# The first feed-forward stage in block form, with the norm's scales on x from the opening on

## The chip, the cores and the metric

The kernel runs on one core of a Trainium2 chip, in one launch. The metric is the time of the launch in microseconds (us) on the device. TensorE (PE in the profile) multiplies, VectorE (DVE) and ScalarE (ACT) work element by element, GpSimd (POOL) does little here beside issuing transfers, and SyncE (SP) issues the transfers of the weights. Each of them executes its own instructions in the order in which they were recorded.

## The reference

A decoder trunk of two layers over 256 tokens with 1024 features, all in float32. Each layer adds four things to the residual h: half a SwiGLU (`ffn1`), a mixer (an S5 state space beside differential attention), a cross attention into 256 memory tokens, and half a second SwiGLU (`ffn2`).

```python
def swiglu(x, w_gate, w_up, w_down):
    return (jax.nn.silu(x @ w_gate) * (x @ w_up)) @ w_down
...
    for l in range(DEPTH):
        h = h + 0.5 * swiglu(rms_norm(h, ffn1_norm[l]), ffn1_w_gate[l], ffn1_w_up[l], ffn1_w_down[l])
        h = h + hybrid_mixer(rms_norm(h, mix_norm[l]), ...)
        h = h + memory_cross_attention(rms_norm(h, xattn_norm[l]), rms_norm(mem, mem_norm[l]), ...)
        h = h + 0.5 * swiglu(rms_norm(h, ffn2_norm[l]), ...)
    return rms_norm(h, final_norm)
```

The inner width of a SwiGLU is 2816. `rms_norm` multiplies by a gain for each feature and by 1/rms for each token. The gain can go onto the rows of the weight or onto the columns of x; the factor of the token is applied behind the product.

## The kernel before

**Split products.** A float32 product is made of three products of a shorter float type: each operand is split into a high part (`whi`, `xh`, made by ScalarE) and a low part (`wlo`, `xl`, the rest, made by VectorE), and TensorE adds hi x hi, lo x hi and hi x lo in PSUM. Every weight that TensorE uses therefore passes ScalarE and then VectorE first.

**The weight stream.** The weights lie in HBM in the order of use, in units of 128x1024 (`stream_plan` lists them). SyncE loads a unit into a `raw` buffer (4 of them), ScalarE makes `whi`, VectorE `wlo` (5 buffers of each). A unit whose norm gain goes onto the weight is split in two halves with the gain as a factor (`split_unit`: forms with `raw,gains`); one without a gain is split whole (`split_whole`). How far the stream runs ahead is bounded by the 5 buffers: a unit's `whi` can begin when TensorE is through with the unit five earlier.

**A feed-forward stage.** The 2816 columns are 11 chunks of 256 gate and 256 up columns. A chunk is four weight units of type A (`P` in the tables below, 12 matmuls of 128x512 each: 2 token tiles x 2 halves x 3 products), and its result (`z`, `sg`) is gated, transposed, split (`gT`) and multiplied by two units of down weights (`D`, 12 matmuls each) some chunks later.

**The pair.** Three of the four stages, all but the first, put two chunks together (`ffn2` does so twice): with two token tiles, two halves of the features and two chunks, a 2x2 block product is made of seven block products instead of eight (`PAIR`: Q3, Q1, Q7, Q6, Q2, Q5, Q4, each two units of 6 matmuls). VectorE forms sums of x blocks (`combos`: `xf`, `ef`, `el`) and of weight blocks in place (`add_block`: `blkX`, `blkY`), and puts the products together (`qs`). Sums of x blocks need the gain on x, so in these stages the residual's preparation scales x with it (`split_gain`, four pieces of 128x128, as the gain is another column for each), and the weights carry none. The order of a stage is a table written out by hand (`SECOND_ONE` for `ffn1`; P chunk, D down rows, S a pair's product):

```python
SECOND_ONE = (
    "P0 P0 P0 P0 P1 P1 P1 P1 P4 D0 P4 D0 "
    "S2 P4 P4 S2 D1 P5 S2 D1 P5 S2 P5 P5 S2 D4 P6 S2 D4 P6 S2 P6 D5 P6 "
    "D5 D3 P7 D3 P7 D2 P7 D2 P7 D6 P8 D6 P8 P8 P8 D7 P9 P9 P9 P9 D7 P10 P10 P10 P10 D8 D8"
)
```

Layer 0's first stage instead goes through `ffn`, eleven plain chunks with the gain on the weights.

**Work beside the stages.** The recording layer is written as tasks (generators) over a clock of estimated costs (`Clock`); the clock decides only in which order instructions are recorded on each engine. `ssm_small` makes the state space's small coefficients for both layers (a chain of about 84 VectorE operations on 128x32, names `sp`, `ex`, `th`, `n`, `fr`, `x`, `pw`, `pr`, `fz`). `tables` makes a layer's larger tables (`tab_states`: `bbar`, `V`, `VT`; `tab_turns`: `ang`, `rnd`, `rot`, `dt`; `tab_out`: `W`, `ks`, `dd`); they use the same buffers (`tA` to `tD`) as the pair's blocks. `setup_mem`, `setup_bias` and `setup_lam` prepare the memory's tiles, the bias and the lambdas. `START` holds the clock times at which `ssm_small` (first value) and the set-up tasks (second) begin. In layer 1 the tables are started when the stage's last pair product has been recorded; in layer 0, which has no pair in `ffn`, from the start of the small chain.

**The opening** (`opening`) covers the first chunk: x comes in by halves (`h` tiles), is transposed by TensorE and split without a gain; the first three weight units are split in halves between these steps; `junk` is the square sum for the norm. The dummy matmuls `pz` keep TensorE busy until the data are there.

Of the kernel before, what the change touches and what calls it, by code (L numbers as in the profile page):

```python
# [11 lines left out]
F32 = mybir.dt.float32  # L12
F32R = mybir.dt.float32r
BF16 = mybir.dt.bfloat16
I32 = mybir.dt.int32
AF = mybir.ActivationFunctionType
# [3 lines left out]
L = 2  # L20
# [11 lines left out]
LAG = 2  # L32
# [13 lines left out]
MMW = 0.8  # L46
START = (45.0, 34.0)
PACE = 2.6
# [63 lines left out]
def stream_plan():  # L112

    plan = []
    for l in range(L):
        def ffn(nm):
            for j in range(NCH):
                for kp in range(4):
                    plan.append((nm + "_gu", l, 4 * j + kp, "A", (nm, l, 2 * kp), 4 if j == 0 and len(plan) >= 4 else 1))
                if j >= LAG:  # L120
                    for f in range(2):
                        plan.append((nm + "_dn", l, 2 * (j - LAG) + f, "B", None, 1))
            for n in range(2 * (NCH - LAG), 2 * NCH):
                plan.append((nm + "_dn", l, n, "B", None, 2 * LAG))

        def second(nm):
            for kind, j, k in second_items(nm):
                if kind == "P":
                    plan.append((nm + "_gu", l, 4 * j + k, "A", None, 4 if j == 0 else 1))
                elif kind == "D":  # L130
                    plan.append((nm + "_dn", l, 2 * j + k, "B", None, 1))
                else:
                    _, loads, operand, add = PAIR[k]
                    for u in range(2):
                        n = [4 * (j + a) + 2 * b + u for _, a, b in loads]
                        plan.append((nm + "_gu", l, n, "S", ((nm, l, j), u, [x[0] for x in loads], operand, add), 1))
            for n in range(2 * (NCH - LAG), 2 * NCH):
                plan.append((nm + "_dn", l, n, "B", None, 2 * LAG))
# [4 lines left out]

        ffn("ffn1") if l == 0 else second("ffn1")
        for c in range(4):
# [239 lines left out]
class Trunk:  # L385
# [319 lines left out]
    def opening(self, evac):  # L705
# [6 lines left out]
        def tr(t, n):  # L712
            p = self.transpose4(self.h[t], [512 * n + 128 * i for i in range(4)])
            o = [a[:, 4 * n:4 * n + 4, :].rearrange("p a b -> p (a b)") for a in self.x[t]]
            self.split(o[0], o[1], p)
            self.tp_done(p)
# [163 lines left out]

    def ffn(self, nm, preps, tail):
        bank = {}
        gT = {}
        accs = None

        def evac(j):
            def f(t, ps):
                c = self.c
                if j:
                    yield tasks[j - 1][t]  # L890
                c.cur.t = max(c.cur.t, self.rt[t])
                sg = self.gp.tile([128, 256], F32, tag="sg", name="sg")
                self.a.activation(sg, ps[:, 0:256], AF.Silu, scale=self.r[t])
                self.v.scalar_tensor_tensor(sg, ps[:, 256:512], self.r[t], sg, op0=ALU.mult, op1=ALU.mult)
                self.mm_done()
                yield
                if j not in bank:
                    yield from self.tp_wait()
                    bank[j] = self.tpt()
                    n = 0  # L900
                else:
                    n = 1
                p = bank[j]
                for f in range(2):
                    o = f * 256 + t * 128
                    self.p.transpose(p[:, o:o + 128], sg[:, f * 128:f * 128 + 128], self.ident)
                if n == 1:
                    hl = self.s4t([128, 2, 512], F32R, name="gT")
                    self.split(hl[:, 0, :], hl[:, 1, :], p)
                    self.tp_done(p)  # L910
                    gT[j] = hl

            return f

        def xs(j, f, t):
            o = f * 256 + t * 128
            return gT[j][:, 0, o:o + 128], gT[j][:, 1, o:o + 128]

        tasks = {}
        for j in range(NCH):  # L920
            if j == 0 and preps is None:
                tasks[j] = self.opening(evac(j))
            else:
                tasks[j] = self.project(nm + "_gu", self.x, evac(j), preps if j == 0 else None)
            if j >= LAG:
                i = j - LAG
                self.c.wait(*tasks[i])
                if accs is None:
                    accs = [self.acc_main(), self.acc_main()]
                for f in range(2):  # L930
                    u = self.unit(nm + "_dn")
                    for t in range(2):
                        self.mm_b(accs[t], *xs(i, f, t), u, i == 0 and f == 0, False)
                    self.free_unit()
        for i in range(NCH - LAG, NCH):
            self.c.wait(*tasks[i])
        base = NCH - LAG
        return self.blocks(nm + "_dn", accs, lambda t, k: xs(base + k // 2, k % 2, t), 2 * LAG, False, True, tail)

    def combos(self, E):  # L940
# [29 lines left out]

    def ffn_second(self, nm, preps, tail, then=None):

# [133 lines left out]
        for kind, j, k in second_items(nm):  # L1106
            if kind == "P":
                if j == 0:
                    if k == 0:
                        tasks[0] = self.project(nm + "_gu", self.x, evac(0, None), preps)  # L1110
                    if k < 3:
# [262 lines left out]
    def tables(self, l, z, tb, first):  # L1374

        st = self.c.spawn(self.chain(first, self.tab_states(l, z, tb), self.tab_turns(l, z, tb)), START[0] if l == 0 else None)
        return st, self.c.spawn(self.chain(st, self.tab_out(l, z, tb)), START[0] if l == 0 else None)

# [440 lines left out]
    def setup(self):  # L1819
# [8 lines left out]
        win = lambda u, s: nc.sync.dma_start(self.raw[u][:, s], io["wst"][u][:, s])  # L1828
        xin(0, lo)
        xin(1, lo, nc.scalar)  # L1830
        nc.scalar.dma_start(self.gains, io["gains"])
        win(0, lo)
# [72 lines left out]
    def run(self):  # L1905
# [5 lines left out]
        small = c.spawn(self.ssm_small(z), START[0])  # L1911
        tables = self.tables(0, z, tb, small)
        c.spawn(self.chain(self.setup_mem(0), self.setup_mem(1), self.setup_bias(), self.setup_lam()), START[1])
        for l in range(L):
            if l == 0:
                preps = self.ffn("ffn1", preps, prep(0.5))
            else:
                tb, tables = {}, []
                preps = self.ffn_second("ffn1", preps, prep(0.5), lambda: tables.extend(self.tables(l, z, tb, None)))
            preps = self.mixer(l, preps, tb, tables, prep(1.0))  # L1920
            preps = self.cross(l, preps, prep(1.0, ("ffn2", l)))
            if l == L - 1:
                self.fn = self.s4t([128, 1024], name="fn")
                self.g.dma_start(self.fn, self.io["final_norm"].to_broadcast([128, 1024]))
            preps = self.ffn_second("ffn2", preps, prep(0.5, ("ffn1", l + 1)) if l < L - 1 else (lambda t, acc: self.final(t, acc, 0.5)))
        c.wait(*preps)
# [69 lines left out]
```

## Time and profile before

| | |
|---|---|
| median of 3 runs | 1193.92 us (1193.57 to 1193.97) |
| profiled execution | 1193.89 us |
| its span, first to last instruction | 1192.1 us |
| PE busy | 1182.4 us (99%) |
| DVE busy | 909.7 us (76%) |
| ACT busy | 707.1 us (59%) |
| POOL busy | 46.7 us (4%) |
| granted TensorE clock | 0.999 |

Times in the profile count from the first instruction. A row of the timeline reads: start in us, duration in us, engine, line, operation, output<-inputs, shapes, count, and in brackets the idle time before it with what ended it. Rows of the same kind that follow each other are merged, and the durations of neighbours overlap, so the price of an instruction in a full queue is the distance of starts and not its duration. A row of windows gives, for each stretch, the busy time and number of instructions of PE, PEld, DVE, ACT and POOL, then the granted clock, the share of the DMA engines and GB/s. Layer 0's first feed-forward stage runs from about 7 us to 208 us of the span, layer 1's from 601 us to 794 us. A line number such as L293 is that of a helper through which all of an engine's operations go, so the names of the tiles tell where an instruction belongs.

### The profile page before, as it was taken

What the parts mean: (1) busy time and instruction counts of PE and PEld (TensorE: products, weight loads), DVE (VectorE), ACT (ScalarE), POOL (GpSimd) and SP (SyncE); (2) the same over time, 40 slices, a digit from 0 to 9 for tenths busy, and PEclk for the clock granted to TensorE, in tenths of its full rate; (3) what the DMA queues carried; (4) which work ended last, traced back from release to release, by engine and by line L of the source; (5) the groups of instructions that cost most, each with busy time, mean ns of one, the idle gap of its engine ahead of it and who ended that gap; (6) DMA issues with size and microseconds to landing.
All of it is one profiled execution on the core that took longest, in us unless ns stands there. A gap on an engine that the chain in (4) does not pass through costs nothing.

```text
span 1192.1 us, 17474 instructions
## 1 busy us (share of the span) xinstructions
PE 1182.4 (99%) x6571; PEld 967.8 (81%) x6571; DVE 909.7 (76%) x1331; ACT 707.1 (59%) x1141; POOL 46.7 (4%) x104
## 2 busy tenths in 40 slices
PE   9999999999999999999999999999999999999997
PEld 7888788877888888888888887888778888888886
DVE  5799676598767688889588985766978575888885
ACT  6665554656866566565466644455767665656553
POOL 1200001000100000000000000010001000000000
PEclk9999999999999999999999999999999999999999
DMA  8656545644544465474557364556436445836542
GB/s 276 227 185 208 156 165 170 195 126 140 177 160 141 159 229 213 142 263 126 176 199 266 123 199 150 176 154 180 150 101 208 150 149 176 305 120 240 183 125 87
DMA packets 59973, 210.90 MB, mean 177 GB/s; under 512 B 7168, under 2 KB 8288, under 8 KB 59888
## 3 DMA queue, kind: packets, MB, share of 16 engines
q1 hardware_dynamic: 56304, 202.92, 52.1%
q0 software_dynamic: 2000, 5.24, 1.6%
q10 hardware_dynamic: 1584, 1.62, 0.6%
q8 instruction: 51, 0.84, 0.3%
q14 instruction: 34, 0.28, 0.1%
HBM read 207.00 MB, written 1.05 MB: 175 GB/s over the span
## 4 chain that ended last, share of the span: by engine, by line
PE 97%; ACT 1%; issue 0%; DMA 0%; DVE 0%; POOLq 0%; POOL 0%; ACTq 0%; DVEq 0%
PE mm L369 50%; PE acc L369 33%; PE tp L369 10%; PE tp L380 5%; DMA gains<-in_gains 0%; ACT junk L330 0%; ACT whi L330 0%; DVE h L293 0%; DVE ang L293 0%; ACT on L330 0%; ACT z L330 0%; DVE wlo L293 0%; POOLq L1992 0%; ACT xh L330 0%; POOL rstd L353 0%
## 5 line engine op out<-in xcount | busy, mean ns | idle before, releaser
L369 PE MATMUL mm<-whi,xh 128*128 128x512 f32 x736 | 295.3, 401 | 1.1 <-ACT whi L330 1.0
L293 DVE TENSOR_TENSOR wlo<-raw,whi 128x1024 fp32r<-128x1024 f32 (+1 forms) x228 | 248.0, 1108 | 51.8 <-ACT whi L330 51.1
L369 PE MATMUL mm<-whi,xl 128*128 128x512 f32 x736 | 287.5, 391 | 0.0
L369 PE MATMUL mm<-wlo,xh 128*128 128x512 f32 x736 | 286.9, 390 | 0.3 <-DVE wlo L293 0.3
L330 ACT ACTIVATE whi<-raw 128x1024 fp32r<-128x1024 f32 (+1 forms) x228 | 214.0, 967 | 54.6 <-PE acc L369 25.6
L293 DVE SCALAR_TENSOR_TENSOR wlo<-raw,gains,whi 128x512 fp32r<-128x512 f32 x280 | 198.7, 746 | 53.0 <-ACT whi L330 50.9
L369 PE MATMUL acc<-whi,gT 128*128 128x512 f32 (+1 forms) x704 | 235.3, 395 | 0.0
L330 ACT ACTIVATE whi<-raw,gains 128x512 fp32r<-128x512 f32 x280 | 184.0, 714 | 10.6 <-PE mm L369 4.6
L369 PEld LDWEIGHTS mm<-whi,xh 128*128 128x128 f32 x736 | 138.2, 188 | 31.7 <-ACT whi L330 1.6
L369 PEld LDWEIGHTS mm<-whi,xl 128*128 128x128 f32 x736 | 138.1, 188 | 29.6 <-DVE xl L293 0.3
L369 PEld LDWEIGHTS mm<-wlo,xh 128*128 128x128 f32 x736 | 138.5, 188 | 26.5 <-DVE wlo L293 1.0
L369 PEld LDWEIGHTS acc<-whi,gT 128*128 128x128 f32 x704 | 132.0, 188 | 26.5
L369 PE MATMUL acc<-wlo,gT 128*128 128x512 f32 (+1 forms) x352 | 136.8, 389 | 0.0
L369 PE MATMUL mm<-whi,mem 128*128 128x512 f32 x256 | 92.4, 409 | 0.2
L330 ACT ACTIVATE z<-mm,rstd 128x256 f32<-128x256 f32 (+1 forms) x70 | 37.8, 547 | 71.7 <-PE mm L369 71.1
L369 PEld LDWEIGHTS acc<-wlo,gT 128*128 128x128 f32 x352 | 66.3, 188 | 12.1
L330 ACT ACTIVATE gT<-tp 128x512 fp32r<-128x512 f32 x44 | 26.4, 599 | 60.4 <-PE tp L380 60.3
L369 PEld LDWEIGHTS mm<-whi,mem 128*128 128x128 f32 x256 | 48.1, 188 | 12.7 <-ACT z L330 1.6
L293 DVE TENSOR_TENSOR wlo<-blkX,whi 128x1024 fp32r<-128x1024 f32 x40 | 48.6, 1220 | 9.9 <-ACT whi L330 9.9
L330 ACT ACTIVATE whi<-blkX 128x1024 fp32r<-128x1024 f32 x40 | 42.0, 1055 | 19.5 <-PE mm L369 7.0
L369 PE MATMUL mm<-wlo,mem 128*128 128x512 f32 x128 | 50.2, 393 | 0.0
L293 DVE TENSOR_TENSOR gT<-tp,gT 128x512 fp32r<-128x512 f32 x44 | 30.3, 688 | 24.6 <-ACT gT L330 24.6
(261 smaller groups left out, 1583.4 us busy)
## 6 DMA issues: line engine op xcount, KB each, us to landing
raw<-in_wst SPq DMA_DIRECT2D x342, 512.0 KB, 4.1
blkX<-in_wst SPq DMA_DIRECT2D x10, 512.0 KB, 4.6
blkP<-in_wst SPq DMA_DIRECT2D x10, 512.0 KB, 7.9
blkY<-in_wst SPq DMA_DIRECT2D x10, 512.0 KB, 9.0
blkQ<-in_wst SPq DMA_DIRECT2D x10, 512.0 KB, 9.6
raw<-in_wst SPq DMA_DIRECT2D x4, 256.0 KB, 5.7
mem<-in_mem POOLq DMA_DIRECT2D x2, 512.0 KB, 4.3
uq<-z ACTq DMA_DIRECT2D x8, 128.0 KB, 5.8
```

The source lines that it names most:

```text
L293: r = getattr(self.e, name)(*a, **k)
L330: r = self.e.activation(out, in_, func, **k)
L369: r = self.e.matmul(out, lhsT, rhs, **k)
L380: r = self.e.transpose(out, in_, ident)
```

## The change

Layer 0's first stage is made as the other three are, with chunks 2 and 3 as a pair; the function `ffn` is removed, and `ffn_second` takes its name. In detail:

- The plan lists the stage by `second`; none of its weight units has a gain, so outside the opening they are split whole.
- The opening's transposed x is split with the gains (`split_gain`) instead of without. For that the gains are fetched first on ScalarE's queue, ahead of the second tile of x.
- `tables` of layer 0 is started by the stage's last pair product, as in layer 1, and then waits for `ssm_small` if that is not through.
- `START` goes from (45, 34) to (60, 110).

```diff
-START = (45.0, 34.0)
+START = (60.0, 110.0)
...
-                    plan.append((nm + "_gu", l, 4 * j + k, "A", None, 4 if j == 0 else 1))
+                    plan.append((nm + "_gu", l, 4 * j + k, "A", None, 4 if j == 0 and len(plan) >= 4 else 1))
...
-        ffn("ffn1") if l == 0 else second("ffn1")
+        second("ffn1")
...
-            o = [a[:, 4 * n:4 * n + 4, :].rearrange("p a b -> p (a b)") for a in self.x[t]]
-            self.split(o[0], o[1], p)
+            self.split_gain(self.x[t], n, p, "ffn1", 0)
...
-    def ffn_second(self, nm, preps, tail, then=None):
+    def ffn(self, nm, preps, tail, then=None):
...
-                        tasks[0] = self.project(nm + "_gu", self.x, evac(0, None), preps)
+                        evac0 = evac(0, None)
+                        tasks[0] = self.opening(evac0) if preps is None else self.project(nm + "_gu", self.x, evac0, preps)
...
-        st = self.c.spawn(self.chain(first, self.tab_states(l, z, tb), self.tab_turns(l, z, tb)), START[0] if l == 0 else None)
-        return st, self.c.spawn(self.chain(st, self.tab_out(l, z, tb)), START[0] if l == 0 else None)
+        st = self.c.spawn(self.chain(first, self.tab_states(l, z, tb), self.tab_turns(l, z, tb)))
+        return st, self.c.spawn(self.chain(st, self.tab_out(l, z, tb)))
...
         xin(0, lo)
+        nc.scalar.dma_start(self.gains, io["gains"])
         xin(1, lo, nc.scalar)
-        nc.scalar.dma_start(self.gains, io["gains"])
...
         small = c.spawn(self.ssm_small(z), START[0])
-        tables = self.tables(0, z, tb, small)
...
-            if l == 0:
-                preps = self.ffn("ffn1", preps, prep(0.5))
-            else:
-                tb, tables = {}, []
-                preps = self.ffn_second("ffn1", preps, prep(0.5), lambda: tables.extend(self.tables(l, z, tb, None)))
+            tb, tables = {}, []
+            preps = self.ffn("ffn1", preps, prep(0.5), lambda: tables.extend(self.tables(l, z, tb, None if l else small)))
```

How instructions move is seen at two places. The first is VectorE where the small chain begins. Before, it stands among half splits with gains of plain chunks (`wlo<-raw,gains,whi`):

```order
L293 SCALAR_TENSOR_TENSOR wlo<-raw,gains,whi 128x512 x5
L293 TENSOR_SCALAR sp<-sp 128x32
L293 TENSOR_SCALAR ex<-sp 128x32
L293 TENSOR_SCALAR ex<-ex 128x32 x2
L293 SCALAR_TENSOR_TENSOR ex<-ex 128x32 x2
L293 TENSOR_SCALAR ex<-ex 128x32
L293 SCALAR_TENSOR_TENSOR ex<-ex 128x32
L293 SCALAR_TENSOR_TENSOR wlo<-raw,gains,whi 128x512 x2
L293 SCALAR_TENSOR_TENSOR ex<-ex 128x32 x5
```

Now it stands inside the pair, behind the block addition and the first split for product Q6 (`blkX`):

```order
L283 TENSOR_TENSOR blkX<-blkX,blkP 128x1024
L283 TENSOR_TENSOR wlo<-raw,whi 128x1024
L283 TENSOR_TENSOR wlo<-blkX,whi 128x1024
L283 TENSOR_SCALAR sp<-sp 128x32
L283 TENSOR_SCALAR ex<-sp 128x32
L283 TENSOR_SCALAR ex<-ex 128x32 x2
L283 SCALAR_TENSOR_TENSOR ex<-ex 128x32 x2
L283 TENSOR_SCALAR ex<-ex 128x32
L283 SCALAR_TENSOR_TENSOR ex<-ex 128x32
L283 TENSOR_TENSOR wlo<-blkX,whi 128x1024
L283 TENSOR_TENSOR wlo<-raw,whi 128x1024
L283 SCALAR_TENSOR_TENSOR ex<-ex 128x32 x5
```

The chain has kept its operations, and what stands between them is now the pair's. It ends behind the pair's last product; 75 of its 84 operations stand ahead of the split of chunk 6's third unit.

The second place is ScalarE in the opening. Before, a gain goes onto each weight half, and x is split in pieces of 512 columns:

```order
L1827 DMA h_109<-in_x 128x512
L1831 DMA gains<-in_gains 128x90
L330 ACT_TABLE_LOAD
L330 ACTIVATE warm<-zero 128x1
L330 ACTIVATE xh<-tp 128x512
L330 ACTIVATE whi<-raw,gains 128x512
L330 ACTIVATE xh<-tp 128x512
L330 ACTIVATE whi<-raw,gains 128x512 x3
L330 ACTIVATE junk,ssq<-h_108 128x1024
```

Now:

```order
L1761 DMA gains<-in_gains 128x90
L1758 DMA h_109<-in_x 128x512
L320 ACT_TABLE_LOAD
L320 ACTIVATE warm<-zero 128x1
L320 ACTIVATE xh<-tp,gains 128x128 x4
L320 ACTIVATE whi<-raw 128x512
L320 ACTIVATE xh<-tp,gains 128x128 x4
L320 ACTIVATE whi<-raw 128x512 x3
L320 ACTIVATE junk,ssq<-h_108 128x1024
```

The two transfers have changed places, the gain has gone from the weights to x, and each piece of x has become four. The places of the steps are the same.

More of the change, by code (lines that the diff above doesn't have):

```diff
@@ L115, in stream_plan @@
     for l in range(L):
[L116 to L124, printed above, removed]
         def second(nm):
@@ L878, in final @@
         yield
[L881 to L900, printed above, removed]
-                else:
[L902 to L938, printed above, removed]
     def combos(self, E):
@@ L1911, in run @@
         small = c.spawn(self.ssm_small(z), START[0])
-        tables = self.tables(0, z, tb, small)
         c.spawn(self.chain(self.setup_mem(0), self.setup_mem(1), self.setup_bias(), self.setup_lam()), START[1])
         for l in range(L):
-            if l == 0:
-                preps = self.ffn("ffn1", preps, prep(0.5))
-            else:
-                tb, tables = {}, []
-                preps = self.ffn_second("ffn1", preps, prep(0.5), lambda: tables.extend(self.tables(l, z, tb, None)))
+            tb, tables = {}, []
+            preps = self.ffn("ffn1", preps, prep(0.5), lambda: tables.extend(self.tables(l, z, tb, None if l else small)))
             preps = self.mixer(l, preps, tb, tables, prep(1.0))
@@ L1924, in run @@
                 self.g.dma_start(self.fn, self.io["final_norm"].to_broadcast([128, 1024]))
-            preps = self.ffn_second("ffn2", preps, prep(0.5, ("ffn1", l + 1)) if l < L - 1 else (lambda t, acc: self.final(t, acc, 0.5)))
+            preps = self.ffn("ffn2", preps, prep(0.5, ("ffn1", l + 1)) if l < L - 1 else (lambda t, acc: self.final(t, acc, 0.5)))
         c.wait(*preps)
```

## The prediction

> **What bounds the kernel now.** I read the page first, then who waited for whom on TensorE, then the timelines of VectorE, ScalarE and TensorE at the three places that the change touches. The page:
>
> ```profile
> span 1192.1 us, 17474 instructions
> PE 1182.4 (99%) x6571; PEld 967.8 (81%) x6571; DVE 909.7 (76%) x1331; ACT 707.1 (59%) x1141; POOL 46.7 (4%) x104
> PE 97%; ACT 1%; issue 0%; DMA 0%; DVE 0%; POOLq 0%; POOL 0%; ACTq 0%; DVEq 0%
> ```
>
> TensorE is busy for all but 9.7 us, and the chain that ended last is 97% PE. Its waits (engine, line, for whom; us in total, times, longest):
>
> ```profile
> PE pz L369 <- DVE zero L293: 1.2, 1, 1.2
> PE mm L369 <- ACT whi L330: 1.0, 1, 1.0
> PE mm L369 <- DVE wlo L293: 0.3, 1, 0.3
> PE tp L380 <- DMA h<-in_x: 0.2, 1, 0.2
> ```
>
> All four lie in the opening; behind it TensorE never waits. So the time is TensorE's row of work: a matmul less is a gain, and any new wait of TensorE is a loss in full. The profiled execution took 1193.89 us, 1.8 us more than its span and 0.03 under the median of 1193.92; I sum against 1193.89.
>
> **The matmuls removed.** Two plain chunks are 8 units of 12 matmuls, 96; the pair is 14 units of 6, 84. Each is 128x512 (TensorE's timeline in the same stage of layer 1):
>
> ```profile
> 687.59 0.39 PE L369 MATMUL mm<-wlo,xh 128*128 128x512 f32 x1
> 690.33 0.39 PE L369 MATMUL acc<-wlo,gT 128*128 128x512 f32 x1
> ```
>
> These two matmuls start 2.74 us apart with eleven others between them, 0.228 each. 12 x 0.228 = 2.7 us less. The transposes stay the same in number: the gain is 2.7.
>
> **The pair beside the small chain.** The operand sums, block additions and extra splits of the pair are VectorE and ScalarE work. Layer 1's first stage has had the same pair, and TensorE waits nowhere there, so by itself this costs nothing. Its cover is VectorE's lead over TensorE. What layer 1 does not have is the state space's chain of small operations (128x32, `ssm_small`), which now stands inside the pair. In the order of the changed kernel it begins right behind the split of the first half of product Q6, and 75 of its 84 operations stand ahead of the split of chunk 6's third unit (`P6`, between the last product, Q4, and the first block of chunk 5's down rows), where the delay is greatest. VectorE executes in order, so each of them delays every split behind it. Layer 1's VectorE over that stretch:
>
> ```profile
> 653.43 1.22 DVE L293 TENSOR_TENSOR wlo<-blkX,whi 128x1024 fp32r<-128x1024 f32 x1
> 655.56 1.23 DVE L293 TENSOR_TENSOR wlo<-blkX,whi 128x1024 fp32r<-128x1024 f32 x1 [0.91 <-ACT whi L330]
> 660.51 1.23 DVE L293 TENSOR_TENSOR wlo<-blkQ,whi 128x1024 fp32r<-128x1024 f32 x1 [1.44 <-ACT whi L330]
> 662.14 0.69 DVE L293 TENSOR_TENSOR qs<-tp,qs 128x512 f32<-128x512 f32 x1 [0.40 <-PE tp L369]
> 678.42 0.48 DVE L293 SCALAR_TENSOR_TENSOR qs<-qs,rstd 128x256 f32<-128x256 f32 x1
> 682.28 1.22 DVE L293 TENSOR_TENSOR wlo<-raw,whi 128x1024 fp32r<-128x1024 f32 x1
> 683.42 0.87 DVE L293 SCALAR_TENSOR_TENSOR qs<-qs,rstd 128x256 f32<-128x256 f32 x2
> ```
>
> Count from 654.65, the end of Q6's first split. VectorE is through with that third unit (the split at 682.28) at 683.42, 28.8 us later. Taking off the three idle pieces (2.75) and the `qs` at 678.42, which the changed order puts behind it (0.4), its work is 25.6 us. TensorE asks for that split at 687.59, 32.9 us after the start. So 7.3 us are free, and the small chain must fit into them.
>
> What one small operation costs is in layer 0 of the profile, where the same chain stands among half splits (VectorE's busy time in a window, then rows of it):
>
> ```profile
> 51.86:88.18 36.32, 36.32 (x170) 29.94 (x169) 32.88 (x117) 19.72 (x32) 0.24 (x1) 1.00 0.67 224
> 51.86 0.28 DVE L293 TENSOR_SCALAR sp<-sp 128x32 f32<-128x32 f32 x1
> 51.94 0.22 DVE L293 TENSOR_SCALAR ex<-sp 128x32 f32<-128x32 f32 x1
> L293 DVE SCALAR_TENSOR_TENSOR ex<-ex 128x32 f32<-128x32 f32 x16 | 3.1, 191 | 0.5
> 54.74 1.08 DVE L293 SCALAR_TENSOR_TENSOR ex<-ex 128x32 f32<-128x32 f32 x5
> 55.74 1.22 DVE L293 TENSOR_TENSOR wlo<-raw,whi 128x1024 fp32r<-128x1024 f32 x1
> 73.72 0.21 DVE L293 TENSOR_TENSOR pw<-mag,cs 128x32 f32<-128x32 f32 x1
> 74.72 1.21 DVE L293 TENSOR_TENSOR wlo<-raw,whi 128x1024 fp32r<-128x1024 f32 x1
> 48.53 3.40 DVE L293 SCALAR_TENSOR_TENSOR wlo<-raw,gains,whi 128x512 fp32r<-128x512 f32 x5 [0.96 <-ACT whi L330]
> 78.16 0.48 DVE L293 SCALAR_TENSOR_TENSOR sg<-mm,rstd,sg 128x256 f32<-128x256 f32 x1 [1.47 <-ACT sg L330]
> ```
>
> Five that feed each other take 1.00 us (0.20 each); the eight from 73.72, side by side, 1.00 (0.125 each). Over the window: 117 instructions, 31 of them large: 17 half splits of 0.66, 4 whole ones of 1.14, 4 gate products of 0.4, four 512-wide lows of 0.6 and two of 0.45 for the lambdas, 20.7 us in all; idle, 1.47 at 78.16 and 0.5 in two shorter waits. That leaves 13.7 us for 86, 0.16 each. So 75 take 12.0, and 12.0 - 7.3 = 4.7 us of wait for TensorE. Behind it the lead comes back without further loss: the splits stand closer, nine small operations are left, and after the pair there is room even with the memory's four splits (0.6 each) and the lambda chain moved there, since layer 1's VectorE waits there for ScalarE:
>
> ```profile
> 726.37 1.23 DVE L293 TENSOR_TENSOR wlo<-raw,whi 128x1024 fp32r<-128x1024 f32 x1 [11.02 <-ACT whi L330]
> ```
>
> Bounds: at 0.09 each (51.86 to 51.94, the nearest pair that does not wait for its forerunner) 75 fit but for nothing, 0; at 191 ns, the mean duration of one, 14.3 - 7.3 = 7.0. I take 4.7, by the window, which is the same chain on the same engine.
>
> The Trainium skill has a rule that speaks for the lower end: Perfetto Trace Analysis, section "Optimizing Scalar/DVE Operations", puts the overhead of an instruction on VectorE at about 60 ns on SBUF. With 32 columns at the 0.96 GHz that VectorE: DVE Perf Modes gives (section "The TRN2 errata"), this is an estimate of 93 ns, 75 take 7.0 and TensorE would not wait at all. The window's 0.16 disagrees.
>
> **The opening.** x is now scaled by the gains as it is split: four pieces of 128x128 in place of one of 128x512, on ScalarE and on VectorE. Rows: eight pieces from the stage where layer 0's second feed-forward begins, then the opening as it is.
>
> ```profile
> 413.88 2.27 ACT L330 ACTIVATE xh<-tp,gains 128x128 fp32r<-128x128 f32 x8 [6.18 <-PE tp L380]
> 415.06 2.25 DVE L293 SCALAR_TENSOR_TENSOR xl<-tp,gains,xh 128x128 fp32r<-128x128 f32 x8 [1.15 <-ACT xh L330]
> 6.52 0.72 ACT L330 ACTIVATE whi<-raw,gains 128x512 fp32r<-128x512 f32 x1 [0.88 <-DMA gains<-in_gains]
> 7.30 0.50 PE L369 MATMUL mm<-whi,xh 128*128 128x512 f32 x1 [1.01 <-ACT whi L330]
> 11.24 0.60 ACT L330 ACTIVATE xh<-tp 128x512 fp32r<-128x512 f32 x1 [0.64 <-PE tp L380]
> 13.07 0.60 ACT L330 ACTIVATE xh<-tp 128x512 fp32r<-128x512 f32 x1 [0.19 <-PE tp L380]
> 13.56 4.39 ACT L330 ACTIVATE whi<-raw,gains 128x512 fp32r<-128x512 f32 x7
> 15.12 0.50 PE L369 MATMUL mm<-wlo,xh 128*128 128x512 f32 x1 [0.28 <-DVE wlo L293]
> gains<-in_gains ACTq DMA_DIRECT2D x1, 45.0 KB, 5.3
> ```
>
> Four pieces hold ScalarE 1.1 us where one took 0.5, so +0.6 for each. Of the two in x's second half the first loses 0.2 to the idle piece at 13.07, so the third weight unit (13.56) starts 1.0 later; without its gain it is 0.1 shorter, and TensorE's wait, which ended at 15.12, ends 0.9 later. With 0.1 from VectorE's longer low parts: +1.0. The start itself: the first weight split (6.52) waited for the gains, whose transfer now goes first on ScalarE's queue, while x's second tile goes second. If the gains land early, up to 0.4 is won; if they again take 5.3 us from an issue 0.44 earlier, the pieces begin at about 6.0, and the first matmul, 1.1 + 0.7 later, starts 0.5 late. Range -0.4 to +1.5, and I take +1.0.
>
> **Moved.** Without gains the first stage's weights are split whole, which is less work; nothing has to cover it. The tables (`tab_states`, `tab_turns`, `tab_out`) wait for the pair, as they do in layer 1, where TensorE waits for none. There is one difference: their last four operations (`dd`, `ks`) now stand on VectorE between the two halves of the first preparation's x, ahead of the mixer. Layer 1 has them before the residual, and a gap at the place where they would now press:
>
> ```profile
> 784.17 0.42 DVE L293 TENSOR_TENSOR dd<-dc,cst 16x256 f32<-16x256 f32 x1
> 784.69 0.42 DVE L293 TENSOR_TENSOR ks<-ks,dd 16x256 f32<-16x256 f32 x1
> 793.29 2.08 DVE L293 SCALAR_TENSOR_TENSOR wlo<-raw,gains,whi 128x512 fp32r<-128x512 f32 x3 [0.81 <-ACT whi L330]
> ```
>
> Four at 0.45 are 1.8 us, 0.8 fall into the gap; 0 to 1.0, and I take 0, since half splits are asked for one after the other. POOL issues the transfers of memory, bias and lambdas behind those of the small chain now; POOL is busy for 46.7 us of the whole span, and the first reader, ScalarE's square of the memory, stands behind the pair, so 0; were it late, ScalarE would hold the weight splits behind it. From the mixer's first chunk on TensorE's order is unchanged.
>
> **Sum.** 1193.9 - 2.7 + 4.7 + 1.0 = 1196.9 us, 0.25% slower. Its own range: 0.14 to 0.18 us per small operation gives a wait of 3.2 to 6.2, so 1195.4 to 1198.4.
>
> **Rivals.** (1) VectorE's slack holds the chain. Its place is the stretch above, its price nothing, and it decides at 7.3/75 = 0.097 us per operation, near the 0.09 of 51.86. Then 1192.2 with the opening at +1.0 and 1190.8 with it at -0.4: faster in the second case. For it: TensorE shows no wait beside the same chain today. Against it: there a unit costs VectorE 1.3 us per 2.7 of TensorE; in the pair a split comes with a block addition or product sum. The Trainium skill's 60 ns (Perfetto Trace Analysis) would give 1192.2 too. (2) The chain costs its full duration, because each operation waits for its forerunner: 0.191 each, 1199.2, and with a late opening 1199.7. For it: most of the first 40 are dependent; against it: the `pw` rows. (3) Half-way: independent rows dominate, 0.125 each, a wait of 2.1, 1194.3. (4) The pair is not the gain it says, because TensorE spends the 2.7 us elsewhere in the stage: the same form in layer 1 runs without a wait, so I leave it 1 in 20, spread over the others.
>
> **Chances.** Forecast 0.55, full duration 0.15, half-way 0.15, slack holds 0.15. A change within 0.2% (2.4 us: 1191.5 to 1196.3) cannot be told from none. Faster than 1191.5 takes rival 1 and a good opening: 0.10. Slower than 1196.3: the forecast's upper 0.40 and rival 2: 0.55. Within: 0.35. The range of 8 in 10 reaches from 1192.2, where rival 1 has its usual opening, to 1199.7, where rival 2 has a late one.
>
> **What would show it.** Right: TensorE waits for `wlo` by some 4 to 5 us in all between about 80 and 105 us, at the units of chunk 6, products Q5 and Q4 and chunk 4's down rows, with VectorE busy without a break there; a wait of about 1 us more near 15 us; no other. Wrong: VectorE idle inside the pair (the chain is cheaper), waits in the mixer (tables or memory late), or a first matmul well before 7 us.

## The result and the profile after

The changed kernel takes 1202.69 us (1201.67 to 1203.08, 4 runs) against 1193.74 (1193.52 to 1193.97) for the kernel before: a ratio of 1.0072, 95% interval 1.006 to 1.0085. It is 8.9 us slower; 3.0 were forecast, and the measured time lies above the range. The profiled execution took 1203.08 us, 9.2 more than the one of before, and the accounts below are made between these two.

The page of the changed kernel, the same three lines as were shown of before:

```profile
span 1201.3 us, 17429 instructions
PE 1184.2 (99%) x6559; PEld 968.9 (81%) x6559; DVE 928.7 (77%) x1333; ACT 707.1 (59%) x1125; POOL 51.5 (4%) x104
PE 94%; DVE 3%; ACT 1%; issue 1%; DMA 0%; POOLq 0%; POOL 0%; ACTq 0%; DVEq 0%
```

TensorE has 12 matmuls less and yet 1.8 us more of busy time: some of them ran slower. The chain that ended last now goes through VectorE for 3% of the span. The waits of TensorE:

```profile
PE tp L359 <- DVE gT L283: 5.4, 1, 5.4
PE mm L359 <- DVE wlo L283: 2.3, 4, 0.7
PE mm L359 <- ACT whi L320: 0.6, 1, 0.6
PE tp L370 <- DMA h<-in_x: 0.4, 1, 0.4
```

The forecast had 4 to 5 us of waits for `wlo` in several pieces. There is one wait of 5.4 us, and it is for `gT`, not for a weight. TensorE's timeline there (start, duration, in brackets the idle time before it):

```profile
84.49 0.48 PE L359 MATMUL mm<-whi,xh 128*128 128x512 f32 x1
85.55 0.50 PE L359 MATMUL mm<-wlo,xh 128*128 128x512 f32 x1 [0.57 <-DVE wlo L283]
88.19 0.40 PE L359 MATMUL mm<-whi,xl 128*128 128x512 f32 x1
93.95 0.80 PE L359 MATMUL tp<-whi,eh 128*128 128x512 f32 x1 [5.36 <-DVE gT L283]
99.21 0.40 PE L359 MATMUL acc<-whi,gT 128*128 128x512 f32 x1
```

Three losses are read from the starts. At 84.49 the next matmul comes 1.06 later where 0.31 is usual behind a transpose: 0.75. At 88.19 it comes 5.76 later instead of 0.23: 5.53. Then the 12 matmuls of product Q5 take from 93.95 to 99.21, 5.26 instead of 2.72: 2.54. The last is the clock, as the stretches show (sum of busy time of TensorE, weight loads, VectorE, ScalarE and GpSimd, then the granted clock):

```profile
84.00:94.00 10.00, 4.06 (x20) 2.74 (x18) 9.93 (x17) 2.93 (x5) 0.00 (x0) 0.92 0.31 85
94.00:99.30 5.30, 5.30 (x13) 4.17 (x14) 5.28 (x23) 1.06 (x1) 0.00 (x0) 0.51 0.45 138
```

Why Q5 waits for `gT`: the products are summed in the two `tp` banks, and one of them still holds chunk 5's transposes. ScalarE had read them at 87.83. VectorE, whose low part `gT` frees the bank, had the following ahead of it:

```profile
87.23 0.60 ACT L320 ACTIVATE gT<-tp 128x512 fp32r<-128x512 f32 x1 [3.41 <-PE tp L370]
86.94 2.35 DVE L283 TENSOR_TENSOR wlo<-blkY,whi 128x1024 fp32r<-128x1024 f32 x2
89.21 1.22 DVE L283 TENSOR_TENSOR blkX<-blkX,blkQ 128x1024 f32<-128x1024 f32 x1
90.34 1.22 DVE L283 TENSOR_TENSOR wlo<-raw,whi 128x1024 fp32r<-128x1024 f32 x1
91.48 1.22 DVE L283 TENSOR_TENSOR blkX<-blkX,blkQ 128x1024 f32<-128x1024 f32 x1
92.61 0.68 DVE L283 TENSOR_TENSOR qs<-qs 128x512 f32<-128x512 f32 x1
93.21 0.68 DVE L283 TENSOR_TENSOR gT<-tp,gT 128x512 fp32r<-128x512 f32 x1
```

Six operations of 6.3 us, none of which TensorE needs before Q5's first product (the first two are Q5's own low parts, which its second product reads), stand ahead of the one that it needs. The opening, ScalarE's rows, one of VectorE and then TensorE's:

```profile
12.35 1.14 ACT L320 ACTIVATE xh<-tp,gains 128x128 fp32r<-128x128 f32 x4 [1.12 <-PE tp L370]
13.37 1.07 ACT L320 ACTIVATE junk<-h 128x1024 bf16<-128x1024 f32 x1
14.40 1.15 ACT L320 ACTIVATE xh<-tp,gains 128x128 fp32r<-128x128 f32 x4
15.40 4.03 ACT L320 ACTIVATE whi<-raw 128x512 fp32r<-128x512 f32 x5
16.63 3.56 DVE L283 TENSOR_TENSOR wlo<-raw,whi 128x512 fp32r<-128x512 f32 x4
16.13 0.49 PE L359 MATMUL mm<-whi,xh 128*128 128x512 f32 x1 [0.60 <-ACT whi L320]
17.37 0.51 PE L359 MATMUL mm<-wlo,xh 128*128 128x512 f32 x1 [0.75 <-DVE wlo L283]
```

The last wait ends at 17.37 instead of 15.12: 2.25 later. The third unit's high part begins 1.84 later than before (15.40 against 13.56), its low part 2.3 later (16.63 against 14.31), because VectorE's own pieces of x (15.59 to 16.63) stand ahead of it. And the first preparation:

```profile
210.54 1.19 ACT L320 ACTIVATE ks<-tp 16x512 f32<-16x512 f32 x2 [9.06 <-PE tp L359]
215.12 0.42 DVE L283 TENSOR_TENSOR ks<-ks,dd 16x256 f32<-16x256 f32 x1
221.48 0.50 PE L359 MATMUL mm<-wlo,xh 128*128 128x512 f32 x1 [0.31 <-DVE wlo L283]
```

TensorE waits there once, for a half split, and its offset to the kernel before grows from 8.4 to 9.0. Two things have made VectorE's splits late. The `dd`/`ks` operations hold it for 1.8 us, from 213.78 to 215.56. And on ScalarE the copies of `ks` wait for TensorE's products of W and stand ahead of the mixer's first high half, which comes at 211.76 (196.70 before); for it VectorE sits idle for 4.2 us. Which of the two makes the 0.6 was not tried. The accounts, in us:

| term | forecast | measured | how |
|---|---|---|---|
| 12 matmuls | -2.7 | -2.7 | 12 x 0.227 |
| pair beside the small chain | +4.7 | +8.8 | 0.75 + 5.53 + 2.54 |
| opening | +1.0 | +2.25 | 17.37 - 15.12 |
| first preparation (`dd`, `ks`) | 0 | +0.6 | 9.0 - 8.4 |
| rest, over 980 us of unchanged order | 0 | +0.25 | |
| sum | +3.0 | +9.2 | |

### The profile page after: what moved, and what is told of

Read it like the earlier page. It is cut to its first block, busy times and chain, and to the rows that moved or that the text cites. A ratio compares the mean times of both kernels' runs of the same rounds, so it can differ in the third digit from the quotient of the medians.

```text
span 1201.3 us, 17429 instructions
## 1 busy us (share of the span) xinstructions
PE 1184.2 (99%) x6559; PEld 968.9 (81%) x6559; DVE 928.7 (77%) x1333; ACT 707.1 (59%) x1125; POOL 51.5 (4%) x104
## 4 chain that ended last, share of the span: by engine, by line
PE 94%; DVE 3%; ACT 1%; issue 1%; DMA 0%; POOLq 0%; POOL 0%; ACTq 0%; DVEq 0%
PE mm L359 46%; PE acc L359 32%; PE tp L359 11%; PE tp L370 5%; DVE wlo L283 1%; ACT junk L320 0%; DMA h<-in_x 0%; ACT xh L320 0%; ACT whi L320 0%; DVE h L283 0%; DVE xl L283 0%; DVE blkY L283 0%; DVE blkX L283 0%; DVE qs L283 0%; DVE ex L283 0%
## 5 line engine op out<-in xcount | busy, mean ns | idle before, releaser
L283 DVE TENSOR_TENSOR wlo<-raw,whi 128x1024 fp32r<-128x1024 f32 (+1 forms) x267 | 291.5, 1113 | 47.9 <-ACT whi L320 47.1
L359 PE MATMUL mm<-whi,xh 128*128 128x512 f32 x704 | 283.2, 402 | 0.7 <-ACT whi L320 0.6
L320 ACT ACTIVATE whi<-raw 128x1024 fp32r<-128x1024 f32 (+1 forms) x267 | 251.2, 971 | 51.4 <-PE acc L359 25.7
L359 PE MATMUL mm<-wlo,xh 128*128 128x512 f32 x704 | 274.8, 391 | 2.3 <-DVE wlo L283 2.3
L359 PE MATMUL mm<-whi,xl 128*128 128x512 f32 x704 | 275.3, 391 | 0.2 <-DVE xl L283 0.2
L283 DVE SCALAR_TENSOR_TENSOR wlo<-raw,gains,whi 128x512 fp32r<-128x512 f32 x192 | 136.5, 748 | 51.9 <-ACT whi L320 51.6
L320 ACT ACTIVATE whi<-raw,gains 128x512 fp32r<-128x512 f32 x192 | 126.5, 715 | 9.1 <-PE mm L359 4.6
L320 ACT ACTIVATE z<-mm,rstd 128x256 f32<-128x256 f32 (+1 forms) x88 | 46.3, 532 | 101.3 <-PE mm L359 100.6
L359 PE MATMUL mm<-whi,mem 128*128 128x512 f32 x256 | 92.4, 409 | 0.2
L320 ACT ACTIVATE whi<-blkX 128x1024 fp32r<-128x1024 f32 x48 | 50.4, 1055 | 28.0 <-PE mm L359 13.7
L283 DVE TENSOR_TENSOR wlo<-blkX,whi 128x1024 fp32r<-128x1024 f32 x48 | 58.5, 1222 | 10.7 <-ACT whi L320 10.7
L359 PEld LDWEIGHTS mm<-whi,mem 128*128 128x128 f32 x256 | 48.1, 188 | 12.7 <-ACT z L320 1.6
## 6 DMA issues: line engine op xcount, KB each, us to landing
blkQ<-in_wst SPq DMA_DIRECT2D x12, 512.0 KB, 10.2
```

Source lines behind the costliest of these rows:

```text
L283: r = getattr(self.e, name)(*a, **k)
L320: r = self.e.activation(out, in_, func, **k)
L359: r = self.e.matmul(out, lhsT, rhs, **k)
```

## The experiments

All are edits of the changed kernel. Ratios are to the kernel before, run on the same chip, with the 95% interval. The theory (A): the small chain inside the pair puts VectorE behind; a bank that is freed late turns this into one wait; the idle TensorE loses its clock.

### The chain behind the pair, and ahead of it

```
-START = (60.0, 110.0)
+START = (104.0, 110.0)      # e1_late
+START = (16.0, 110.0)       # e2_early
```

> The small chain begins behind the pair (104 instead of 60 in the order's time), nothing else is edited. Theory A (the chain inside the pair puts VectorE behind, and TensorE pays 0.75 + 5.53 us of waiting and 2.54 us at half clock there): all 8.8 us go, 1203.1 - 8.8 = 1194.3 us, with no wait of TensorE between 80 and 110 us and the clock at 1.00; a little more if the tables, which follow the chain, come late for the mixer. Theory B (the pair by itself is too much for VectorE or for the two banks in this stage, wherever the chain stands): the wait for gT before product Q5 stays, 1200 to 1203 us.

> The small chain begins at 16 in the order's time, so that it stands ahead of and in the first half of the pair. Theory A: VectorE has idle pieces there (1.45, 1.98 and 0.71 us at 47 to 59 us) and a lead of 3 to 6 us, so the chain fits: 1194.3 us, no wait for gT. Theory B: the waits of the pair stay, 1200 to 1203 us. Between them, if the chain costs the same lag wherever it stands in the stage: about 1198 to 1199, in waits for wlo of under 2 us each, without a fall of the clock.

Late: 1197.35 us, 1.0028 (1.0017 to 1.004). Early: 1203.22 us, 1.0076 (1.0062 to 1.009). The longest wait of the late one and its stretch beside the pair, then the longest wait of the early one and the clock behind it:

```profile
PE tp L370 <- DVE yT L283: 2.1, 1, 2.1
84.00:100.00 16.00, 16.00 (x74) 13.21 (x73) 14.44 (x18) 9.78 (x12) 0.00 (x0) 1.00 0.44 135
```
```profile
PE mm L359 <- DVE z L283: 3.9, 1, 3.9
38.00:42.60 4.60, 4.60 (x12) 3.53 (x12) 4.42 (x12) 0.00 (x0) 0.00 (x0) 0.50 0.96 340
```

With the chain behind the pair TensorE is busy without a break from 84 to 100 us at full clock: all 8.8 us of the pair are gone, and theory B (the pair is too much by itself) falls. But 3.1 us are lost anew in the mixer: two short waits at 207 and 210 us, where the late tables stand among the splits, and the one for `yT` at 307 us. That the late tables cause this last wait too was not traced. The six runs took 1196.2 to 1196.3 us three times and 1198.4 to 1198.5 three times, and the median lies between; the profiled one took 1198.46, and in it the clock is at 0.50 for 3.4 us behind the wait for `yT`, which costs 1.7. That the shorter runs kept their clock would fit, and is not shown. Ahead of the pair the chain stands among the operand sums (`xf`, `ef`, `el`), delays the gate product `z` of chunk 1, and the loss is as large as in the pair: my count of idle pieces there left out that `z` frees a bank, too. None of the three places tried has room for the chain's 13.7 us.

### Work in the wait

```
+                if preps is None and (j, k) == (6, 0):
+                    for i in range(22):
+                        self.p.e.matmul(ps[0], self.zz, u[0][:, 0:512], start=False, stop=False)
                 self.free_unit()
```

> 22 matmuls of a zero tile (they add zero to chunk 6's sum) stand ahead of product Q5, where TensorE waited 5.4 us: some 5.0 us of work in the wait. Theory A (the slow 12 matmuls of Q5 are the clock that falls because TensorE was idle): they take 0.227 us each in place of 0.427, the granted clock in the rows is 1.00, and 2.5 us come back: 1200.5 us. Rival (they are slow for another reason, such as VectorE's or the banks' traffic, or the time comes back as a wait behind them): 0.427 us each as before or a new wait of 2.5 us, 1203.1 us.

1200.22 us (1199.98 to 1200.39), 1.0052 (1.004 to 1.0065): 2.5 us less than the changed kernel, although TensorE has 5 us of work more. The stretch with the zero matmuls, and the one behind:

```profile
88.00:93.00 5.00, 5.00 (x23) 3.89 (x21) 5.00 (x6) 0.60 (x3) 0.00 (x0) 1.00 0.16 32
93.00:98.00 5.00, 4.75 (x21) 3.78 (x21) 5.00 (x19) 3.57 (x4) 0.00 (x0) 1.00 0.49 179
```

The clock stays at 1.00 and Q5's matmuls stand 0.23 apart. So the 2.5 us are the clock, and it fell because TensorE was idle: shown.

### `gT` ahead of the block operations

```
-            if u >= self.nfree + N_W or
+            if u > least and 32 <= u < 36 and not self.open or u >= self.nfree + N_W or
```

(`open` is set where chunk 5's low part has been issued.)

> The splits of units 32 to 35 are held back until the low part of chunk 5's gT stands in VectorE's order, so gT stands ahead of five block operations instead of behind them; the chain stays inside the pair. Theory A in its full form (VectorE's total lag of 5.5 us is real; its place in the queue makes it one wait, longer by 0.8, and lets the clock fall, 2.5): TensorE's waits are spread over Q5, P6 and Q4, none over 3 us, no slow clock, 4 to 5.5 us in all: 1198.5 to 1200 us. Rival C (the queue place alone is the fault; VectorE is not behind otherwise): hardly any wait is left, about 1194.5 to 1196 us.

1197.38 us, 1.0028 (1.0018 to 1.0039): 5.3 us less, from the order of VectorE's work alone. Its waits in the pair:

```profile
85.28 0.50 PE L359 MATMUL mm<-wlo,xh 128*128 128x512 f32 x1 [0.58 <-DVE wlo L283]
89.84 0.51 PE L359 MATMUL tp<-wlo,eh 128*128 128x512 f32 x1 [0.76 <-DVE wlo L283]
93.24 0.50 PE L359 MATMUL acc<-wlo,gT 128*128 128x512 f32 x1 [0.35 <-DVE wlo L283]
```

Some 3 us of short waits at full clock, three of them shown, at P6, Q5 and the down rows: what the forecast described, and less than its 4.7, because the held splits also move the chain's last operations behind those of chunk 6. The time lies between the two expectations; the queue place is most of the loss, not all.

### The chain on GpSimd

`ssm_small` and what it calls take GpSimd's operations instead of VectorE's; a multiply-add becomes two. The first two runs differ in START (16 and 40), and the second also has the opening's order of the next section.

> The small chain runs on GpSimd (each multiply-add as two operations, the reciprocal and the absolute value left on VectorE), begun at 16 in the order's time; the pair, the opening and the tables stay. Theory A (the chain's 84 places in VectorE's order are what the pair cannot carry): no wait for gT, no slow clock, and with the chain's results in time for the tables 8.8 us come back: 1194.3 us. Rival (the chain slows the pair from GpSimd too, because operations of the two engines on the same memory hold each other up, or its results come too late from the slower engine): VectorE's whole splits grow beyond their 1.13 us in the rows, or the mixer waits, and 1197 us or more.

> The chain on GpSimd (begun at 40) together with another order in the opening: the third weight unit is split ahead of x's second half, and the two sums of squares stand behind the opening's splits. If the two losses are independent, 1194.3 less the 1.5 to 2.0 us of the opening: 1192.3 to 1192.8 us, below the kernel before. If what the opening gains is lost again at the next wait: 1194 us.

1226.42 us, 1.0272 (1.0258 to 1.0286), and 1206.13 us, 1.0105 (1.0091 to 1.0119): both much slower, for a reason that no expectation had. VectorE in the first:

```profile
42.91 0.19 DVE L283 SCALAR_TENSOR_TENSOR x<-th 128x32 f32<-128x32 f32 x1 [20.08 <-POOL th L343]
```

One small operation was left on VectorE, the absolute value of `th`. The planner took GpSimd to be done sooner, and VectorE stood 20 us in front of it with all splits queued behind (11.7 us in the second run). This tells nothing about the pair. The next run has the planner's cost right:

```
+        self.g.c.engine("pool", 0.5)
...
+        yield
         self.v.scalar_tensor_tensor(x1, th, -1.0, th, op0=ALU.mult, op1=ALU.max)
```

> As in the earlier run with the chain on GpSimd, but the planner takes 0.5 us for each of its operations there, so that the absolute value on VectorE and the sines on ScalarE stand in their orders only where GpSimd's results are there (before, they stood some 20 us too early and held both engines). Theory A: VectorE has no chain in the pair, no wait for gT and no slow clock: 1194.3 us. Rival (GpSimd's operations and VectorE's hold each other up): VectorE's whole splits above 1.13 us apart, waits in the pair, 1196 us or more.

1194.76 us, 1.0007 (0.9998 to 1.0016), 0.5 above the 1194.3 of theory A. There is no wait for `gT`; what is left of new waits is small:

```profile
PE mm L381 <- DVE wlo L283: 1.3, 3, 0.7
PE mm L381 <- DVE z L283: 0.8, 2, 0.6
PE tp L392 <- ACT up L320: 0.6, 1, 0.6
```

The rival's effect is there, but small: VectorE's whole splits of `raw` between 60 and 108 us take 1250 ns on average here and 1213 in the changed kernel.

### The opening

In the first run x is split in one piece, without the gains (they are left out). In the second the gains stay, and the order is another:

```
         self.split_next()
-        stat(0)
+        self.split_next()
+        self.split_next()
         tr(0, 1)
-        stat(1)
...
-        self.split_next()
         mm(0, 3)
         mm(1, 3)
-        self.split_next()
...
+        stat(0)
+        stat(1)
         out = []
```

> In the opening x is split in one piece of 128x512 as in the kernel before; the gains of layer 0's first norm are left out of the computation altogether. Everything else is the changed kernel's, the gains' transfer ahead of x's second tile included. Theory D (the opening's 2.25 us are ScalarE and VectorE time of the four pieces): TensorE's matmul behind the last wait of the opening comes at 15.2 to 15.6 us in place of 17.37, and the total is 1.7 to 2.1 us lower, 1201.1 us. Rival E (the later landing of x's second tile, behind the gains): it stays at 16.8 us or later, 1202.5 to 1203 us.

> The changed kernel with the other order in the opening alone (third unit split ahead of x's second half, sums of squares later); the gains stay. Theory D2 (ScalarE's queue in the opening sets the third unit, and 1.3 us of squares and 2.3 us of pieces stand ahead of it): the matmul behind the opening's last wait comes at 15.4 to 15.9 us instead of 17.37, total 1201.2 us. Rival (the third unit's weights land too late to be split earlier): 16.8 us or later and 1202.5 us or more.

1202.24 us, 1.0069 (1.0055 to 1.0083), and 1201.9 us, 1.0068 (1.0055 to 1.0081): no difference to the changed kernel that these runs can tell, though the opening is repaired. Without the gains the matmul behind the last wait comes at 14.23, with the other order the wait is not there at all and the matmul that stood at 18.64 stands at 16.72 (16.38 in the kernel before). The long wait of the first, and the third unit's split on ScalarE in the second:

```profile
PE tp L359 <- DVE gT L283: 7.8, 1, 7.8
```
```profile
11.20 1.16 ACT L320 ACTIVATE whi<-raw 128x512 fp32r<-128x512 f32 x2 [1.01 <-DMA raw<-in_wst]
```

This split fills the gap of 1.12 us at 12.35 in which ScalarE had waited for TensorE's transposes. So the order of the opening made the 2.25 us, 1.84 of it in ScalarE's queue (theory D2) and 0.4 in VectorE's, and rival E, the transfer, falls: it is as in the changed kernel in both runs. But a TensorE that comes 2 us earlier to a bank which VectorE frees at 93 us waits 7.8 us there instead of 5.4. VectorE's `gT` ends at about the same time (Q5 starts at 93.06 and 93.37 against 93.95), so the opening's term and the pair's could not simply be added: the later wait had swallowed the first. (In the second run, the later squares also cost a new wait of 1.3 us for `z`.)

### Without the pair

Layer 0's first stage gets the list of eleven plain chunks again (`P0`..., `D0 D0`, 96 matmuls instead of 84), START (45, 34).

> Layer 0's first stage without the pair: eleven plain chunks in the old order (12 matmuls more than the changed kernel), chain and tables begun at 45 and 34 as before; x with gains and the new opening stay. Theory A (the pair beside the chain costs 8.8 - 2.7 = 6.1 us and the opening 2.2): 1193.8 + 2.2 = 1196.0 us, the only waits of TensorE in the opening. Rival (the gains on x, not the pair, put VectorE behind): 1199 us or more, with waits beyond 20 us.

1195.72 us, 1.0016 (1.0007 to 1.0025), with waits in the opening alone, the largest group of them:

```profile
PE mm L363 <- DVE wlo L287: 1.4, 3, 0.7
```

Without the pair the chain costs nothing, as in the kernel before; what is left is the opening. The gains on x do not put VectorE behind.

### The version that keeps the gain

Chain on GpSimd as in e9_pool2; in the opening the third unit ahead of x's second half, the first sum of squares where it was, the second behind the fourth unit; `dd` ahead of W. Then the spacing:

```
-PACE = 2.6
+PACE = 1.8       # e12_pace; e13_mem also START[1] 110 -> 200
```

> The chain on GpSimd as in the run beside this one, the opening with the third weight unit split ahead of x's second half and the second sum of squares behind the fourth unit, and the two products dd computed before W instead of between x's halves. If the parts add up: 1194.3 less 1.9 (opening, by the matmul times of the earlier opening run: 16.72 against 18.64 us) less 0.3 to 0.6 (dd): 1191.8 to 1192.2 us, faster than the kernel before by 0.15%. If VectorE's queue takes the opening's gain as it did in the two opening runs: 1193.5 to 1194 us.

> The best version so far (chain on GpSimd, other opening) with the spacing factor of the order, PACE, at 1.8 instead of 2.6, so that the products W of the tables stand ahead of the first residual instead of between the splits of the mixer's first units. There TensorE waited 0.8 us for wlo at 207 us and 0.9 us for xl at 210 us. If the W products (four of 0.75 us in 4 us) are the cause, those 1.7 us go: 1192.5 us. If the splits are late for another reason, the waits stay and it is 1194.2 us.

> As the run beside this one, and the memory's four splits and the lambdas begin at 200 instead of 110, behind the tables. By the W theory 1192.5 us again, with the waits at 207 and 210 us gone; if the memory's splits, now among the mixer's (where a half split comes every 0.7 us), press instead, a new wait of 0.5 to 2 us behind 215 us and 1193 to 1194.5 us.

| run | us | ratio (interval) |
|---|---|---|
| e10_best | 1194.21 | 1.0002 (0.9993 to 1.001) |
| e12_pace | 1191.15 | 0.9978 (0.9969 to 0.9987) |
| e13_mem | 1197.32 | 1.0027 (1.0017 to 1.0036) |

TensorE and VectorE at the preparation in e10_best, where the expectation had no cost:

```profile
211.50 0.50 PE L381 MATMUL mm<-whi,xl 128*128 128x512 f32 x1 [0.75 <-DVE xl L283]
208.50 0.82 DVE L283 TENSOR_TENSOR Wt<-bc,pw 128x640 f32<-128x640 f32 x1
210.76 1.28 DVE L283 TENSOR_TENSOR xl<-tp,xh 128x512 fp32r<-128x512 f32 x2
```

The tables' products stood among the splits. With the closer spacing they are through ahead of the residual, and the waits of the whole program are

```profile
PE pz L381 <- DVE zero L283: 1.2, 1, 1.2
PE mm L381 <- DVE wlo L283: 0.8, 2, 0.5
```

less than in the kernel before. It is 2.65 us faster than the kernel before, about the 2.7 of the 12 matmuls, and 1.3 below its own expectation of 1192.5, for which no run gives the reason. In the profiled execution TensorE is 3.2 us ahead when the preparation of the second tile begins (its transposes at 208.79 against 211.95) and 3.1 at the end; 0.5 of that is won in the opening (the matmul at 16.38 in the kernel before stands at 15.91), the rest is the 12 matmuls. With the memory's splits moved into the mixer the same kernel loses 6 us there (e13_mem, eleven runs from 1195.8 to 1199.3 us), 2.1 of them at `yT` again: of the two places tried, the one behind the pair has room for that work.

## Why the prediction was wrong, step by step

**The 12 matmuls: right.** 2.7 us, by TensorE's rows; e12_pace shows the whole of it as a gain.

**The price of the chain: nearly right.** The 75 operations ahead of chunk 6's third unit took 12.5 us in the changed kernel (12.7 by the distances of starts between 66.05 and 103.10, less 0.2 in which VectorE waits for TensorE), 0.167 each, where the window gave 0.16 and 12.0. The estimate from the Trainium skill that was weighed (Perfetto Trace Analysis, section "Optimizing Scalar/DVE Operations": 60 ns and the columns, 93 ns) is out by a factor of 1.8 here; the window had spoken against it. The lag was also nearly right. That unit's low part and TensorE's use of it:

```profile
103.10 1.16 DVE L283 TENSOR_TENSOR wlo<-raw,whi 128x1024 fp32r<-128x1024 f32 x1
107.60 0.39 PE L359 MATMUL mm<-wlo,xh 128*128 128x512 f32 x1
```

Without its three losses TensorE would have come at 107.60 - 8.82 = 98.8; the low part ended at 104.26, 5.5 late where 4.7 were forecast; 0.5 of the difference is the price.

**Where TensorE pays: wrong, and this is the step that failed.** "Where the delay is greatest" was looked for among the weight units alone. TensorE also waits for banks. Layer 1's `gT` at this place, and its Q5, in the profile of before:

```profile
674.42 0.68 DVE L293 TENSOR_TENSOR gT<-tp,gT 128x512 fp32r<-128x512 f32 x1
676.03 0.39 PE L369 MATMUL tp<-whi,eh 128*128 128x512 f32 x1
```

The room there is 676.03 - 675.10 = 0.9 us, not 7.3. In the changed order 47 operations of the chain stand ahead of `gT`: at 0.16, 7.5 us. Less VectorE's idle 2.75 us and the 0.9, that is 3.9 us late. And the new order has `gT` two whole operations further back, a raw split and a block sum, 2.3 us: 6.2 in all, measured 0.75 + 5.53. So it could have been worked out, but that it comes out so closely is luck: these 47 mostly feed each other and took 8.7 us, and the new order has a product sum of 0.6 behind `gT` that layer 1 has ahead of it, which together give 6.7. The waits are 0.8 us more than VectorE's lag further on, and nearly all in one piece. The sign that was named, VectorE busy without a break, did appear (9.93 of the 10 us from 84 to 94); waits for `wlo` in several pieces did not.

**That a wait costs its length: wrong.** It was "a loss in full", nothing more. A long one also takes the clock: 2.54 us here, 2.5 by e3_warm. The Trainium skill, TensorE: Matmul & The Clock Gate, section "Part 1: The HAM clock gate", states that an idle window of about 3.4 us puts TensorE on half its clock; the prediction did not draw on it, and forecast its 4 to 5 us as several waits. The traces agree in part: behind this wait of 5.4 us the clock did fall, but it also fell 2.8 us after the last matmul's start in e2_early, and behind a wait of 2.15 us in e1_late (below).

**The opening: the size was off, 2.25 for 1.0.** The working gave the third unit 1.0 on ScalarE, and left TensorE's own delay out. But x's pieces wait for TensorE's transposes, which come 1.1 later by then, and the pieces and the second sum of squares between them then follow without a pause: 1.84. VectorE's longer low parts, put at 0.1, cost 0.4. e8_open shows that the order was the cause. It also shows that the sum was not a sum: while VectorE frees the bank late, the opening costs nothing that can be measured.

**`dd` and `ks`: 0.6, inside the stated 0 to 1.0.** Taking 0 was the lower end. The working looked at VectorE's four operations alone; ScalarE's copies of `ks`, which also moved in front of the mixer, were not in it, and how much of the 0.6 is theirs stays open.

**The rivals.** None had it. Rival 1 (the slack holds the chain) and 3 fall by the 5.5 us; rival 2 (full duration) had the right direction for a wrong reason, since the operations did not get dearer. Rival 4 is out: with the chain on GpSimd and the tables out of the way (e12_pace) the gain is there.

## What to carry to other kernels

When work is put on an engine beside a pipeline, list everything that this engine releases, banks as well as operands, and find the smallest lead of them; the weight splits had 7.3 us and the bank 0.9. Some 14 us of small operations on a busy engine need a place, not only a start time: all three start times lost, and moving the work to an idle engine, with the tables' order closed up, kept the gain. Waits of one engine that follow each other need not add: here the later one took up what the earlier one gave.

## What the runs showed of the hardware

TensorE's granted clock fell to 0.50 some 2.8 to 5.0 us after the start of its last matmul: 2.8 in e2_early (wait of 3.9 us), 2.9 in e7_nogain, 4.2 in the changed kernel, 4.6 in e8_open, 5.0 in e6_poolopen. These moments are worked out from the mean clock of a stretch, as in the changed kernel: 0.92 over 10 us is 1.6 us at half, so from 92.4. Single waits of 1.3 us (e8_open) and 1.7 us (e6_poolopen) left it at full. In e1_late a wait of 2.15 us was enough in the profiled execution, with four transposes behind it; the clock fell 0.5 us after they had begun:

```profile
306.00:308.00 2.00, 0.72 (x5) 0.72 (x6) 1.86 (x2) 1.51 (x3) 0.49 (x1) 0.94 0.44 135
308.00:310.00 2.00, 2.00 (x6) 1.52 (x6) 2.00 (x5) 1.63 (x3) 0.00 (x0) 0.50 0.50 174
```

It came back after 3.3 (e6_poolopen) to 5.9 us (e5_pool) of work. The stretch at 0.50, worked out in the same way, lasted 3.4 us in e1_late, 6.8 in the changed kernel, e2_early, e6_poolopen and e8_open, and 10.2 in e7_nogain: one, two and three times 3.4. What a wait cost beyond its length is half of the time that TensorE worked in that stretch: 2.6 of the 5.2 us from 93.95 in the changed kernel. The changed kernel's runs also spread over 1.4 us, and those of e3_warm, whose clock does not fall in the profiled execution, over 0.4; that the moment of the fall makes this spread is a guess.

GpSimd's 128x32 operations depend on what VectorE does. In e5_pool VectorE stood idle until 42.91:

```profile
42.96 0.29 POOL L343 TENSOR_SCALAR fr<-th 128x32 f32<-128x32 f32 x1
44.86 1.03 POOL L343 TENSOR_TENSOR fr<-fr,n 128x32 f32<-128x32 f32 x1
```

Beside whole splits of VectorE one mostly takes 1.0 us and more, beside an idle VectorE 0.25 to 0.3. The chain of 13.7 us on VectorE took 50 us there in e6_poolopen (each multiply-add as two operations) and 90, with its waits for the other engines, in e12_pace; layer 0's first stage has that time.
